# Moving one ScalarE conversion behind four copies in the attention of a two-layer decoder

## The chip, the cores and the metric

The kernel runs on one core of a Trainium2 chip, as one program in one launch. The metric is device time in microseconds (us), the median of several executions; less is better. A separate execution was taken with the hardware profiler, and all rows below come from it.

The engines have short names in the rows. PE is the matrix engine TensorE, and PEld its weight loads, which run beside the matmuls. DVE is VectorE, ACT is ScalarE, POOL is GpSimd, and SP is the engine whose queue issues the weight DMAs. Each engine takes its own instructions strictly in the order in which they were queued, and waits at the first one that isn't ready.

## What is computed

Two layers over 256 positions of width 2048, in float32. Layer 0 is a retention and a short convolution with one input and one output projection. Layer 1, in which the change lies, is windowed attention:

```python
def odd_mixer(h, w_in, q_norm_w, k_norm_w, sinks, w_out, pos):
    proj = h @ w_in
    q, k, v, gate = jnp.split(proj, [ATTN_WIDTH, ATTN_WIDTH + KV_WIDTH, ATTN_WIDTH + 2 * KV_WIDTH], axis=-1)
    q = rope(rms_norm(q.reshape(b, s, ATTN_Q_HEADS, ATTN_HEAD_DIM), q_norm_w), pos)
    k = rope(rms_norm(k.reshape(b, s, ATTN_KV_HEADS, ATTN_HEAD_DIM), k_norm_w), pos)
    o = swa_sinks(q, k, v, sinks).reshape(b, s, ATTN_WIDTH)
    return (o * jax.nn.silu(gate)) @ w_out
```

There are 32 query heads of 64 columns and 4 key/value heads, so four groups of eight query heads share a key head.

## The kernel before

**Products.** Every projection is cut into chunks of 512 output columns, and a chunk into 8 pieces of 256 input rows. A piece is one weight DMA of 512 KB into a tile `raw` (in the rows `woq`, `wog`, `woo` by the chunk's kind: query, gate, output projection). ACT writes its rounded upper part `wh` (`whoq`, `whog`, `whoo`, line 165), DVE the rest `wl = raw - wh` (line 166), and PE adds three products for each of two row blocks and two halves of the piece: 12 matmuls a piece (line 143). The activations are split the same way into an `h` and an `l` tile. There are five buffers each of `raw`, `wh` and `wl`, so ACT converts pieces that PE comes to five pieces later, and the conversion of one piece waits until PE has used the piece five before it.

**Background work.** Work that isn't a projection is written as generators on a list `pending`; after every piece of a chunk, `feed` runs one step of the first of them. So the attention of a group lies in pieces between the products, and all engines take it in that order.

**Layer 1.** The chunks run in the order keys and values, query 0, gate 0, query 1, gate 1, query 2, gate 2, query 3, gate 3, and then the output projection. When a query chunk is done, `attention(g, ...)` (line 589) is put on the list. Its first steps are: the scales `rr` (line 713), then for each row block `t` the turning of the queries, then what an earlier group left over, then the scores.

- `turn_q(t, qs)` (line 594): for each half `j`, PE transposes four heads into a PSUM tile `qt` (line 598), and ACT copies it into `qT[j]` (the rows say `q1T`, line 599). The PSUM tiles `qt` come from the pool `tp`, which has two buffers: the transposes for `t = 1` can't start before the copies for `t = 0` have been read out.
- `finish(j)` (line 747): turns the gated output `og[j]` of a half into the activations of the output projection. ACT writes `ah` (line 749, in the rows `a2h`), and POOL (or, for the last half of all, DVE) writes `al = og - ah` (line 751, `a2l`).
- `late` (line 587): for groups 0 to 2 the second `finish` isn't run by the group itself but left on this list; the next group runs it after its two turnings of queries:

```python
        for t in range(T):
            turn_q(t, qs[t])
            yield
        while late:
            late.popleft()()
        yield
```

The text sets the order only in part. The instructions of the engines are put in a queue by a scheduler, which keeps to what depends on what and otherwise chooses; it queued this conversion on ACT ahead of the copies of the turned queries, though the text runs it behind them. With four groups there are three such places, in the gate chunks of groups 1, 2 and 3. Group 0 goes through the same turning of queries with nothing on `late`.

In the rows `og` is the gated output, whose last step is the multiplication by the gate on DVE (line 709); `gv` is the gate, `qs` the split queries before the turning, `s` the scores, `pt` transposed probabilities, `psog` and `psoq` the PSUM tiles of gate and query chunks.

Of the kernel before, what the change touches and what calls it, by code (L numbers as in the profile page):

```python
# [10 lines left out]
AF = mybir.ActivationFunctionType  # L11
# [46 lines left out]
def hybrid_kernel(  # L58
# [13 lines left out]
    nc = tc.nc  # L72
# [17 lines left out]
    def f32(a):  # L90
        return a.bitcast(F32)
# [474 lines left out]
    def queries(g, ps):  # L566

        rr = op2.tile([P, T, 8], F32, tag="rr", name=f"rr{g}")
        qs, rs = [], []
        for t in range(T):  # L570
            ss = head_ss(f"q{g}{t}", ps[t], 8, t)
            rot = rope1(f"q{g}{t}", "q", ps[t].rearrange("p (h d) -> p h d", h=8), 8, t)
            rs.append(rsqrt_mean(f"q{t}", ss, HD, 8))
            qs.append(split_q(g, t, rot))
        pending.append(attention(g, rr, rs, qs))
# [11 lines left out]
    late = deque()  # L587

    def attention(g, rr, rs, qs):
        ah, al = act2.new()  # L590
        qT = [op2.tile([P, 4, T, P], F32R, tag="qT", name=f"q1T{g}{j}") for j in range(2)]
        mx, pr, nm, es, den = {}, {}, {}, {}, {}

        def turn_q(t, qs):
            for j in range(2):
                tr = tp.tile([P, 4, P], F32R, tag="tp", name=f"qt{g}{t}{j}")
                for h in range(4):
                    nc.tensor.transpose(tr[:, h, :], qs[j][:, h].rearrange("p a d -> p (a d)"), identr)  # L598
                nc.scalar.activation(qT[j][:, :, t, :], f32(tr), AF.Copy)

        def scores(j, h):

# [112 lines left out]
            )  # L715
        yield
        for t in range(T):
            turn_q(t, qs[t])
            yield
        while late:  # L720
            late.popleft()()
        yield
        for j in range(2):
            mx[j] = op2.tile([P, T, 4], F32, tag="mx", name=f"mx{g}{j}")
# [173 lines left out]
```

## Time and profile before

| what | us |
|---|---|
| runs, median of 3 | 803.12 |
| runs, lowest and highest | 802.4 and 803.49 |
| profiled execution, own time | 804.01 |
| its span, first to last instruction | 802.3 |
| PE busy in it | 791.9 (99%) |
| ACT busy in it | 419.5 (52%) |
| DVE busy in it | 501.7 (63%) |
| POOL busy in it | 62.4 (8%) |

The profiled execution took 804.01 us, of which the rows cover the span of 802.3 us; its own time is 0.89 us above the median. Busy time counts an instruction from its start to its modelled end. The matmuls overlap: one starts about 0.23 us after the one before, while each is shown with some 0.39 us. So a short gap between two rows of PE is shorter than what PE lost there, and starts are compared with starts.

### The profile page before, as it was taken

Reading aid. Unit: us, or ns where it says so; the run is one execution under the profiler, and the core shown is the slowest. Engines: PE = TensorE matmul, PEld = TensorE weight load, DVE = VectorE, ACT = ScalarE, POOL = GpSimd, SP = SyncE. Lnnn points to the kernel's source line nnn. Section 1 sums busy time; section 2 is a strip of 40 time slices with the busy share of each in tenths; the row PEclk is TensorE's granted clock in tenths of the full one; section 3 lists DMA queues with packets and bytes.
Section 4 is the critical chain, followed back from the end, with each engine's and each line's share of the span. In section 5 each row is a group of like instructions: output and inputs, shape, how many; then the busy total and the mean of one; then the engine's idle time right before and its main releaser. Section 6 shows DMA issues by size and latency. Waiting matters only on the chain.

```text
span 802.3 us, 10004 instructions
## 1 busy us (share of the span) xinstructions
PE 791.9 (99%) x3660; PEld 654.1 (82%) x3660; DVE 501.7 (63%) x742; ACT 419.5 (52%) x665; POOL 62.4 (8%) x61
## 2 busy tenths in 40 slices
PE   8999999999999999999999999999999999999998
PEld 6888888888888888888888888888878788788886
DVE  6566454664545475445856664877977977777651
ACT  6753434443444434443445443758658678586431
POOL 0000000000000000000000000420500601401000
PEclk9999999999999999999999999999999999999999
DMA  8966645555455655555555555462474454445750
GB/s 310 398 226 229 207 134 185 183 188 197 138 184 190 203 184 183 186 200 192 172 194 176 184 184 193 132 210 84 166 221 132 134 184 157 147 143 174 231 171 26
DMA packets 41088, 147.09 MB, mean 183 GB/s; under 512 B 4560, under 2 KB 4944, under 8 KB 40784
## 3 DMA queue, kind: packets, MB, share of 16 engines
q1 hardware_dynamic: 40752, 146.23, 54.5%
q8 instruction: 28, 0.46, 0.2%
q10 hardware_dynamic: 288, 0.24, 0.2%
q14 instruction: 20, 0.16, 0.1%
HBM read 144.36 MB, written 2.10 MB: 183 GB/s over the span
## 4 chain that ended last, share of the span: by engine, by line
PE 89%; DVE 4%; POOL 3%; issue 2%; ACT 1%; DMA 1%; DVEq 0%; ACTq 0%; POOLq 0%
PE pse L143 44%; PE psoo L143 11%; PE pseo L143 11%; PE psoq L143 10%; PE psog L143 3%; PE psokv L143 3%; POOL rq L225 2%; DVE wlog L166 1%; POOL qs L583 1%; PE pt L674 1%; DVE og L707 1%; DMA sml<-in_small 1%; PE qt L598 1%; PE s L606 0%; DVE og L709 0%
## 5 line engine op out<-in xcount | busy, mean ns | idle before, releaser
L166 DVE TENSOR_TENSOR wle<-we,whe 128x1024 fp32r<-128x1024 f32 (+1 forms) x129 | 156.3, 1217 | 148.6 <-ACT whe L165 148.3
L165 ACT ACTIVATE whe<-we 128x1024 fp32r<-128x1024 f32 (+1 forms) x129 | 135.6, 1052 | 173.9 <-PE pse L143 159.2
L143 PE MATMUL pse<-whe,a0h 128*128 128x512 f32 x512 | 200.0, 396 | 1.3 <-ACT whe L165 1.3
L143 PE MATMUL pse<-whe,a0l 128*128 128x512 f32 x512 | 198.3, 391 | 0.0
L143 PE MATMUL pse<-wle,a0h 128*128 128x512 f32 x512 | 197.8, 390 | 0.0
L143 PEld LDWEIGHTS pse<-whe,a0h 128*128 128x128 f32 x512 | 96.5, 189 | 22.4 <-ACT whe L165 2.9
L143 PEld LDWEIGHTS pse<-whe,a0l 128*128 128x128 f32 x512 | 96.7, 189 | 20.6
L143 PEld LDWEIGHTS pse<-wle,a0h 128*128 128x128 f32 x512 | 96.7, 189 | 19.8
L165 ACT ACTIVATE wheo<-weo 128x1024 fp32r<-128x1024 f32 x32 | 33.9, 1061 | 48.3 <-PE pseo L143 32.7
L166 DVE TENSOR_TENSOR wloo<-woo,whoo 128x1024 fp32r<-128x1024 f32 x32 | 39.5, 1239 | 27.8 <-ACT whoo L165 27.7
L166 DVE TENSOR_TENSOR wleo<-weo,wheo 128x1024 fp32r<-128x1024 f32 x32 | 39.2, 1225 | 27.5 <-ACT wheo L165 27.5
L165 ACT ACTIVATE whoo<-woo 128x1024 fp32r<-128x1024 f32 x32 | 33.9, 1062 | 37.9 <-PE psoo L143 32.7
L166 DVE TENSOR_TENSOR wloq<-woq,whoq 128x1024 fp32r<-128x1024 f32 x32 | 40.0, 1252 | 21.0 <-ACT whoq L165 20.5
L143 PE MATMUL psog<-whog,a1h 128*128 128x512 f32 x128 | 51.0, 398 | 0.0
L143 PE MATMUL psoq<-whoq,a1h 128*128 128x512 f32 x128 | 50.8, 397 | 0.0
L143 PE MATMUL pseo<-wheo,c0h 128*128 128x512 f32 x128 | 50.8, 397 | 0.0
L143 PE MATMUL psog<-wlog,a1h 128*128 128x512 f32 x128 | 50.0, 391 | 0.5 <-DVE wlog L166 0.5
L165 ACT ACTIVATE whoq<-woq 128x1024 fp32r<-128x1024 f32 x32 | 33.9, 1060 | 31.6 <-PE psoq L143 14.0
L143 PE MATMUL psoo<-whoo,a2h 128*128 128x512 f32 x128 | 50.3, 393 | 0.0
L143 PE MATMUL psoq<-wloq,a1h 128*128 128x512 f32 x128 | 50.0, 391 | 0.0
L143 PE MATMUL pseo<-wleo,c0h 128*128 128x512 f32 x128 | 50.0, 390 | 0.0
L143 PE MATMUL psoo<-whoo,a2l 128*128 128x512 f32 x128 | 50.0, 390 | 0.0
(182 smaller groups left out, 1246.3 us busy)
## 6 DMA issues: line engine op xcount, KB each, us to landing
we<-in_w SPq DMA_DIRECT2D x127, 512.0 KB, 3.3
weo<-in_w SPq DMA_DIRECT2D x32, 512.0 KB, 3.2
woq<-in_w SPq DMA_DIRECT2D x32, 512.0 KB, 4.2
wog<-in_w SPq DMA_DIRECT2D x32, 512.0 KB, 3.3
woo<-in_w SPq DMA_DIRECT2D x32, 512.0 KB, 4.2
wokv<-in_w SPq DMA_DIRECT2D x8, 512.0 KB, 3.2
x<-in_xr SPq DMA_DIRECT2D x2, 1024.0 KB, 9.5
out_y<-y SPq DMA_DIRECT2D x7, 256.0 KB, 4.5
```

Of the source, the lines that this page charges most:

```text
L143: nc.tensor.matmul(self.ps[t], self.act(kt)[a][:, t * P : (t + 1) * P], w[:, k * N : (k + 1) * N], start=self.n[t] == 1, stop=self.n[t] == ...
L165: nc.scalar.activation(wh[:, ws], raw[:, ws], AF.Copy)
L166: nc.vector.tensor_tensor(out=wl[:, ws], in0=raw[:, ws], in1=f32(wh[:, ws]), op=ALU.subtract)
L225: nc.gpsimd.tensor_tensor(out=r, in0=v, in1=mhalf[:, :width], op=ALU.pow)
L583: nc.gpsimd.tensor_tensor(out=q[:, :, 1, :], in0=aj, in1=f32(q[:, :, 0, :]), op=ALU.subtract)
L598: nc.tensor.transpose(tr[:, h, :], qs[j][:, h].rearrange("p a d -> p (a d)"), identr)
L674: nc.tensor.transpose(tr[:, h, :], pr[j][:, h, t, :], ident)
L707: nc.vector.tensor_tensor(out=og[half[e], :, ts], in0=o[half[e], :, e, :], in1=sh[half[e]], op=ALU.add)
```

## The change

`turn_q` hands back its last ACT instruction, the copy for `j = 1`, and the left-over work is run inside a block that adds an order without a semaphore: every instruction that the block creates on the engine of `copy` (ACT) is queued behind `copy`. `finish(1)` creates one instruction on ACT, the conversion `a2h`, and one on POOL, `a2l`, which waits for `a2h` in any case.

```diff
                     nc.tensor.transpose(tr[:, h, :], qs[j][:, h].rearrange("p a d -> p (a d)"), identr)
-                nc.scalar.activation(qT[j][:, :, t, :], f32(tr), AF.Copy)
+                copy = nc.scalar.activation(qT[j][:, :, t, :], f32(tr), AF.Copy)
+            return copy.ins
...
         for t in range(T):
-            turn_q(t, qs[t])
+            copy = turn_q(t, qs[t])
             yield
         while late:
-            late.popleft()()
+            with tc.issue_after(copy):
+                late.popleft()()
```

The queues of PE, DVE, POOL and SP hold the same instructions in the same order as before. On ACT three instructions move, one in each of groups 1 to 3. The lines behind the edit are numbered one or two higher afterwards.

ACT's queue in the gate chunk of group 1, before. `whoq_0` to `whoq_3` convert the first pieces of query chunk 2, ahead of their use; `q1T` are the copies of the turned queries of group 1, `a2h` is the left-over conversion of group 0, `sh` a part of its output, `gv` the gate of group 1:

```order
L705 ACTIVATE sh_4599<-ov_4576 64x256 x2
L165 ACTIVATE whoq_0_4752<-woq_0_4751 128x1024
L749 ACTIVATE a2h_4033<-og_4324 128x512
L165 ACTIVATE whoq_1_4793<-woq_1_4792 128x1024
L599 ACTIVATE q1T_4607<-qt_4647 128x4x128
L599 ACTIVATE q1T_4608<-qt_4653 128x4x128
L165 ACTIVATE whoq_2_4832<-woq_2_4831 128x1024
L599 ACTIVATE q1T_4607<-qt_4677 128x4x128
L599 ACTIVATE q1T_4608<-qt_4683 128x4x128
L165 ACTIVATE whoq_3_4880<-woq_3_4879 128x1024
L560 ACTIVATE gv_4744<-psog_0_4530,r1h 128x512
```

The same place of ACT's queue after the change:

```order
L706 ACTIVATE sh_4599<-ov_4576 64x256 x2
L165 ACTIVATE whoq_0_4752<-woq_0_4751 128x1024
L165 ACTIVATE whoq_1_4793<-woq_1_4792 128x1024
L599 ACTIVATE q1T_4607<-qt_4647 128x4x128
L599 ACTIVATE q1T_4608<-qt_4653 128x4x128
L165 ACTIVATE whoq_2_4832<-woq_2_4831 128x1024
L599 ACTIVATE q1T_4607<-qt_4677 128x4x128
L599 ACTIVATE q1T_4608<-qt_4683 128x4x128
L751 ACTIVATE a2h_4033<-og_4324 128x512
L165 ACTIVATE whoq_3_4880<-woq_3_4879 128x1024
L560 ACTIVATE gv_4744<-psog_0_4530,r1h 128x512
```

`a2h` has moved past two weight conversions and four copies, and now stands between the last copy and `whoq_3`. Nothing else changed places.

ACT's queue in the gate chunk of group 3, before, where the pieces converted ahead are those of the first output chunk (`whoo`):

```order
L165 ACTIVATE whoo_0_5902<-woo_0_5901 128x1024
L749 ACTIVATE a2h_5179<-og_5472 128x512
L165 ACTIVATE whoo_1_5943<-woo_1_5942 128x1024
L599 ACTIVATE q1T_5755<-qt_5795 128x4x128
L599 ACTIVATE q1T_5756<-qt_5801 128x4x128
L165 ACTIVATE whoo_2_5982<-woo_2_5981 128x1024
L599 ACTIVATE q1T_5755<-qt_5825 128x4x128
L599 ACTIVATE q1T_5756<-qt_5831 128x4x128
```

And after:

```order
L165 ACTIVATE whoo_1_5943<-woo_1_5942 128x1024
L599 ACTIVATE q1T_5755<-qt_5795 128x4x128
L599 ACTIVATE q1T_5756<-qt_5801 128x4x128
L165 ACTIVATE whoo_2_5982<-woo_2_5981 128x1024
L599 ACTIVATE q1T_5755<-qt_5825 128x4x128
L599 ACTIVATE q1T_5756<-qt_5831 128x4x128
L751 ACTIVATE a2h_5179<-og_5472 128x512
L165 ACTIVATE whoo_3_6030<-woo_3_6029 128x1024
```

The conversion made the same move here.

## Rows read from the trace of the kernel before

**Rows 1.** The profile's page: busy time of each engine, the TensorE clock granted in 40 slices of the span (tenths, 9 is 90% or more), and the shares of the chain of work that ended last.

```profile
PE 791.9 (99%) x3660; PEld 654.1 (82%) x3660; DVE 501.7 (63%) x742; ACT 419.5 (52%) x665; POOL 62.4 (8%) x61
...
PEclk9999999999999999999999999999999999999999
...
PE 89%; DVE 4%; POOL 3%; issue 2%; ACT 1%; DMA 1%; DVEq 0%; ACTq 0%; POOLq 0%
```

**Rows 2.** Who PE waited for, whole program: us in total, times, longest us.

```profile
PE qt L598 <- ACT q1T L599: 3.2, 3, 1.1
PE warm L195 <- DVE zero L192: 1.6, 1, 1.6
PE pse L143 <- ACT whe L165: 1.3, 1, 1.3
PE psog L143 <- DVE wlog L166: 0.5, 1, 0.5
```

**Rows 3.** PE in order of time, in the gate chunk of group 1 around the turning of the queries: start us, us, engine, line, operation, output and inputs, count, and in brackets the idle time before and what ended it. The row of 584.81 is the last matmul of the chunk's sixth piece, that of 587.13 the first of its seventh.

```profile
581.36 0.39 PE L143 MATMUL psog<-whog,a1l 128*128 128x512 f32 x1
581.59 0.79 PE L598 MATMUL qt<-identr,qs 128*128 128x128 f32 x8
...
584.81 0.39 PE L143 MATMUL psog<-whog,a1l 128*128 128x512 f32 x1
586.29 1.00 PE L598 MATMUL qt<-identr,qs 128*128 128x128 f32 x8 [1.09 <-ACT q1T L599]
587.13 0.47 PE L143 MATMUL psog<-whog,a1h 128*128 128x512 f32 x1
```

**Rows 4.** The same view in the gate chunks of groups 2 and 3.

```profile
639.79 0.39 PE L143 MATMUL psog<-whog,a1l 128*128 128x512 f32 x1
641.25 0.99 PE L598 MATMUL qt<-identr,qs 128*128 128x128 f32 x8 [1.07 <-ACT q1T L599]
642.08 0.47 PE L143 MATMUL psog<-whog,a1h 128*128 128x512 f32 x1
...
694.71 0.39 PE L143 MATMUL psog<-whog,a1l 128*128 128x512 f32 x1
696.17 1.00 PE L598 MATMUL qt<-identr,qs 128*128 128x128 f32 x8 [1.07 <-ACT q1T L599]
697.01 0.47 PE L143 MATMUL psog<-whog,a1h 128*128 128x512 f32 x1
```

**Rows 5.** ACT in order of time, in the gate chunk of group 1. The four `whoq` rows from 579.06 on are `whoq_0` to `whoq_3`, the two `q1T` rows the pairs of copies for `t = 0` and `t = 1`.

```profile
579.06 1.06 ACT L165 ACTIVATE whoq<-woq 128x1024 fp32r<-128x1024 f32 x1 [0.30 <-PE psog L143]
584.08 0.63 ACT L749 ACTIVATE a2h<-og 128x512 fp32r<-128x512 f32 x1 [3.96 <-DVE og L709]
584.62 1.04 ACT L165 ACTIVATE whoq<-woq 128x1024 fp32r<-128x1024 f32 x1
585.57 1.07 ACT L599 ACTIVATE q1T<-qt 128x512 fp32r<-128x512 f32 x2
586.53 1.05 ACT L165 ACTIVATE whoq<-woq 128x1024 fp32r<-128x1024 f32 x1
587.47 1.08 ACT L599 ACTIVATE q1T<-qt 128x512 fp32r<-128x512 f32 x2
590.23 1.06 ACT L165 ACTIVATE whoq<-woq 128x1024 fp32r<-128x1024 f32 x1 [1.67 <-issue]
592.22 1.37 ACT L560 ACTIVATE gv<-psog,r1h 128x512 f32<-128x512 f32 x2 [0.93 <-PE psog L143]
```

**Rows 6.** Who ACT waited for, whole program, one row of it: us in total, times, longest us.

```profile
ACT a2h L749 <- DVE og L709: 11.8, 3, 4.0
```

**Rows 7.** DVE in order of time at the same place. The rows of line 166 are the rests of the last three gate pieces and of `whoq_0`, `whoq_1` and `whoq_3`.

```profile
578.41 2.89 DVE L166 TENSOR_TENSOR wlog<-wog,whog 128x1024 fp32r<-128x1024 f32 x2
...
582.22 1.23 DVE L166 TENSOR_TENSOR wlog<-wog,whog 128x1024 fp32r<-128x1024 f32 x1
583.37 0.68 DVE L709 TENSOR_TENSOR og<-og,gT 128x512 f32<-128x512 f32 x1
583.97 1.22 DVE L166 TENSOR_TENSOR wloq<-woq,whoq 128x1024 fp32r<-128x1024 f32 x1
585.70 1.70 DVE L166 TENSOR_TENSOR wloq<-woq,whoq 128x1024 fp32r<-128x1024 f32 x1 [0.51 <-ACT whoq L165]
...
591.32 1.23 DVE L166 TENSOR_TENSOR wloq<-woq,whoq 128x1024 fp32r<-128x1024 f32 x1 [2.48 <-ACT whoq L165]
```

**Rows 8.** PE and then ACT in order of time at the turning of the queries of group 0, where nothing is left over.

```profile
531.10 0.39 PE L143 MATMUL psog<-whog,a1l 128*128 128x512 f32 x1
531.33 0.80 PE L598 MATMUL qt<-identr,qs 128*128 128x128 f32 x8
531.97 0.47 PE L143 MATMUL psog<-whog,a1h 128*128 128x512 f32 x1
...
531.58 1.06 ACT L165 ACTIVATE whoq<-woq 128x1024 fp32r<-128x1024 f32 x1 [0.97 <-PE psog L143]
```

**Rows 9.** Who the weight loads of PE waited for, whole program, one row of it.

```profile
PEld qt L598 <- issue: 4.4, 3, 1.5
```

**Rows 10.** POOL in order of time, from the split of the queries of group 1 to its next work behind `a2l`.

```profile
577.73 2.49 POOL L583 TENSOR_TENSOR qs<-aq,qs 128x256 fp32r<-128x256 f32 x2
584.79 1.52 POOL L751 TENSOR_TENSOR a2l<-og,a2h 128x512 fp32r<-128x512 f32 x1 [4.57 <-ACT a2h L749]
611.33 0.64 POOL L685 TENSOR_SCALAR_AFFINE_SELECT uh<-ph 128x512 fp32r<-128x512 f32 x1 [25.02 <-ACT ph L678]
```

**Rows 11.** SP in order of time: the weight DMAs for `woq_1` and `woq_2` being issued; and the time from issue to landing of the DMAs of `woq` between 560 and 600 us.

```profile
567.78 0.33 SPq L164 DMA_DIRECT2D woq<-in_w  x1
579.68 0.33 SPq L164 DMA_DIRECT2D woq<-in_w  x1
...
DMA to landing us min/median/max: 3.7/4.5/4.9
```

**Rows 12.** Two pieces of the chain that ended last, in order of time: start us, us, what. They are the fourth piece of query chunk 2, the first that uses `whoq_3`, and the fifth piece of the first output chunk, the first that reads `a2h` and `a2l` of group 2.

```profile
603.95 2.75 PE psoq L143 x12
...
717.02 2.79 PE psoo L143 x12
```

## The prediction

> **What bounds the kernel now.** I read the page first. PE is busy for 791.9 of 802.3 us at the full clock in every slice (the 2.4 GHz level), and the chain that ended last lies on PE for 89% [rows 1]. So an edit on ACT is worth what PE stands still for, and nothing else. The next view is therefore who PE waited for. In the whole program there are four lines, and the longest is the one that touches this change: the transposes of the turned queries (line 598) waited three times for the copies on ACT (line 599), 3.2 us together [rows 2]. The third view is the order of time on PE around one of them, in the gate chunk of group 1: the transposes for `t = 0` follow the matmul ahead of them without a gap, those for `t = 1` come at 586.29, with 1.09 us idle ahead, put down to `q1T` [rows 3]. Groups 2 and 3 show the same with 1.07 us [rows 4].
>
> The fourth view says why the copies were late. ACT ended `whoq_0` at 580.12 and then stood for 3.96 us, until DVE had finished `og`, since `a2h` was at the head of its queue. Only then came `whoq_1` and, at 585.57, the first copies [rows 5]. That wait is there three times, 11.8 us in all [rows 6]. The fifth view, DVE, shows why `og` is late: its last step stands behind three weight rests and ends at 583.37 + 0.68 = 584.05 [rows 7]. So the chain is DVE `og`, ACT `a2h`, `whoq_1`, copies, PE transposes. A control stands in the same trace: group 0 has nothing left over, and its second transposes follow at 531.33, 0.23 us after the matmul ahead [rows 8].
>
> **What the wait costs.** Idle time on PE's row isn't the loss, since matmuls overlap. I take start to start, from the last matmul of the sixth piece to the first of the seventh. Group 1: 587.13 - 584.81 = 2.32 us [rows 3]. Groups 2 and 3: 642.08 - 639.79 = 2.29 and 697.01 - 694.71 = 2.30 [rows 4]. Group 0, without a wait: 531.97 - 531.10 = 0.87 [rows 8]. The excess is 1.45 + 1.42 + 1.43 = 4.30 us. It is more than three idle gaps (1.09 + 1.07 + 1.07 = 3.23 [rows 3, 4]) because the transposes themselves spread out, 1.00 instead of 0.80 us, while they wait for the second copy.
>
> The weight loads give a second measure: those of the transposes stood for 4.4 us in three waits [rows 9]. The Trainium skill, Perfetto Trace Analysis, section Identifying the Most-Contended Engine, says that the busy share of matmuls is a poor measure for PE, because pipelined instructions look different in the trace, and that the busy share of the weight loads should be used instead. By PE's own row the gain would end at 3.2 us, by that rule at 4.4; the starts, which are neither, agree with the rule.
>
> **Removed.** The wait of `a2h` ahead of `whoq_1`. What releases `whoq_1` next? Its buffer is that of the fifth gate piece, whose last matmul starts at 581.36 and is shown for 0.39 [rows 3], so 581.75. In group 0 a conversion that waited for PE started at 531.58, against 531.10 + 0.39 = 531.49 [rows 8], so I add 0.09: 581.84. Its weights were issued at 567.78 and land in 3.7 to 4.9 us [rows 11], long before. `whoq_1` takes 1.04, and the two copies end 586.64 - 584.62 = 2.02 after its start [rows 5], so 583.86. The transposes that they read are done by 581.59 + 0.79 = 582.38 [rows 3]. The second transposes can start at 584.81 + 0.23 = 585.04 as in group 0, and the last copy is out 1.18 us before. So the whole excess should go, not a part of it.
>
> **Moved.** `a2h` goes behind `whoq_2` and the second copies. `whoq_2` waits for the sixth piece: 584.81 + 0.39 + 0.09 = 585.29. Its weights, issued at 579.68, land by 584.2 to 584.6 [rows 11]: some 0.7 us of cover, and if that is gone the copies behind it slip, which nothing reads before the chunk is done; its gate starts at 592.22 - 1.45 = 590.8 [rows 5], 3.4 us later. It takes 1.05, the copies are over 587.47 + 1.08 - 586.53 = 2.02 after its start [rows 5], at 587.31, and `a2h` comes at about 587.2, long after `og` is ready at 584.05. It adds 584.62 - 584.08 = 0.54 us to the queue [rows 5], to 587.8. Behind it stand `whoq_3` and the gate `gv`. `whoq_3` started at 590.23 after 1.67 us of idle time [rows 5]; 1.45 us earlier that is 588.78, so `a2h` lies in idle time with 1 us to spare. If that cover weren't there, it would cost from 0 to 3 x 0.54 = 1.6 us; I take 0, because PE needs `whoq_3` only at 603.95 [rows 12], and its rest ends at 591.32 + 1.23 [rows 7].
>
> `a2l` on POOL follows 0.71 us after the start of `a2h` and takes 1.52 [rows 10], so it ends near 589.5. POOL's next work is at 611.33 [rows 10], so nothing queues behind it. The readers of `a2h` and `a2l` are the output chunks: for group 2, whose conversion moves to 587.2 + 697.01 - 587.13 = 697.1 [rows 3, 4] on the old times, the first is at 717.02 [rows 12]. Also held longer, by about 3 us, is the buffer of `og`; no instruction between there and 611.33 on POOL's queue needs it. On DVE the rest of `whoq_1` took 1.70 us beside `a2l`, against 1.22 for the one ahead [rows 7, 10]; `a2l` will now lie in the 2.5 us in which DVE waits for `whoq_3`. Neither way does PE see it. SP's queue has no new entry; the weight DMAs that wait for `wloq_1` go out about 1 us earlier.
>
> **What is late next.** Behind each place the next wait of PE in layer 1 before was at the next place [rows 2], and what ACT and DVE do in between is started by PE's chunks, so it moves with PE. I expect the full 4.30 us to arrive at the end.
>
> **The sum.** The profiled execution's own time is 804.01 us, its span 802.3. 804.01 - 4.30 = 799.7, with a span near 798.0. Against the median of the runs, 0.89 us lower: 803.12 - 4.30 = 798.8 us, 0.54% faster.
>
> **The rivals.**
>
> *Only part comes.* The copies could come early and PE still wait, for a semaphore from the copies or for `whoq_1` starting later than PE's fifth piece allows. For it: `whoq_1` was never seen without `a2h` ahead of it. Against it: group 0 has the same queue and no gap [rows 8], and 1.18 us are to spare. Half the excess left gives 803.12 - 2.15 = 801.0 us. Chance 0.08.
>
> *It doesn't do what it says, or it comes back.* The wait named could have been another: if `whoq_1` were released at about 584.6 by something that the row doesn't name, the copies come when they came before, and the time stays at 803.1. Or DVE and POOL, whose chain of `og`, rests and split queries between two chunks is long, hold PE later for what was gained. Against the first stands the row itself, which names DVE's `og`, and `og` ends 0.03 us before `a2h` starts; against the second, that the split queries for `t = 1` are done at 577.73 + 2.49 = 580.2 [rows 10], nearly 5 us before their transposes, and the rests of the gate pieces at 583.4 [rows 7], before PE's seventh piece at 585.7. Chance 0.05, 803.1 us.
>
> *Slower: the wait moves with the instruction.* `a2h` at its new place is again the head of ACT's queue; if `og` weren't ready there, `whoq_3`, the gate and the copies of the scores would stand behind it. If PE then paid the whole wait of ACT (3.96 us, three times, instead of the 1.45 that reach it now), the time would be 803.12 + 11.9 - 4.3 = 810.7 us. It decides from the point where `og` ends later than `whoq_3` can start, 588.8; the row has `og` at 584.05 [rows 7], 4.7 us before, and DVE's work ahead of it isn't touched. Chance 0.02.
>
> **How the numbers follow.** The forecast has 0.85, the rivals 0.08, 0.05 and 0.02. About 0.2% (1.6 us) is what a measurement of this kernel can tell from no change; forecast and the first rival lie beyond it: faster 0.93, same 0.05, slower 0.02. For the range I take the two bounds of the excess against the spread of the runs of before: 802.4 - 4.4 = 798.0, and 803.49 - 3.23 = 800.3.
>
> **What would show it.** Right: PE's wait for `q1T` is gone from the list of waits, start to start at the three places is 0.87 us, `a2h` has no wait for `og`, `whoq_1` starts right after the fifth piece, ACT idles before `whoq_3` for about 1 us, the span is near 798.0. Wrong: a gap of PE before the second transposes that names something other than a copy (part only); an idle time of ACT before `a2h` (slower); new lines of waits of PE in layer 1 that add up to what was gained (it comes back).

## The result and the profile after

| | before | after |
|---|---|---|
| median of 6 runs each, us | 803.32 | 799.02 |
| lowest and highest, us | 802.4 and 803.84 | 797.76 and 799.53 |
| profiled execution, own time, us | 804.01 | 798.12 |
| its span, us | 802.3 | 796.4 |

The changed kernel is faster by 4.30 us; the ratio is 0.9944, with a 95% interval from 0.9931 to 0.9957. The forecast was 798.8 us, a gain of 4.30, with a range from 798.0 to 800.3.

Who PE waited for, whole program, in the changed kernel (us in total, times, longest us):

```profile
PE warm L195 <- DVE zero L192: 1.5, 1, 1.5
PE pse L143 <- ACT whe L165: 1.4, 2, 0.9
PE psog L143 <- DVE wlog L166: 0.5, 1, 0.5
```

Against [rows 2] one line is gone, the wait of the turning transposes for the copies, and no new one stands in layer 1. PE in order of time around the second transposes of groups 1, 2 and 3 (start us, us, engine, line, operation):

```profile
583.28 0.39 PE L143 MATMUL psog<-whog,a1l 128*128 128x512 f32 x1
583.51 0.79 PE L598 MATMUL qt<-identr,qs 128*128 128x128 f32 x8
584.14 0.47 PE L143 MATMUL psog<-whog,a1h 128*128 128x512 f32 x1
...
636.79 0.39 PE L143 MATMUL psog<-whog,a1l 128*128 128x512 f32 x1
637.02 0.79 PE L598 MATMUL qt<-identr,qs 128*128 128x128 f32 x8
637.65 0.47 PE L143 MATMUL psog<-whog,a1h 128*128 128x512 f32 x1
...
690.29 0.39 PE L143 MATMUL psog<-whog,a1l 128*128 128x512 f32 x1
690.53 0.79 PE L598 MATMUL qt<-identr,qs 128*128 128x128 f32 x8
691.16 0.47 PE L143 MATMUL psog<-whog,a1h 128*128 128x512 f32 x1
```

From the last matmul of the sixth piece to the first of the seventh it is now 0.86, 0.86 and 0.87 us, where [rows 3, 4] had 2.32, 2.29 and 2.30, and group 0 had 0.87 [rows 8]. The three differences are 1.46 + 1.43 + 1.43 = 4.32 us. ACT in order of time at the place in group 1:

```profile
580.26 1.06 ACT L165 ACTIVATE whoq<-woq 128x1024 fp32r<-128x1024 f32 x1 [1.66 <-PE psog L143]
581.22 1.07 ACT L599 ACTIVATE q1T<-qt 128x512 fp32r<-128x512 f32 x2
583.71 1.06 ACT L165 ACTIVATE whoq<-woq 128x1024 fp32r<-128x1024 f32 x1 [1.42 <-PE psog L143]
584.68 1.07 ACT L599 ACTIVATE q1T<-qt 128x512 fp32r<-128x512 f32 x2
585.63 0.63 ACT L751 ACTIVATE a2h<-og 128x512 fp32r<-128x512 f32 x1
587.21 1.06 ACT L165 ACTIVATE whoq<-woq 128x1024 fp32r<-128x1024 f32 x1 [0.94 <-ACT a2h L751]
```

The two weight conversions now wait for PE, 1.66 and 1.42 us, as that of group 0 did; the first copies end at 582.29, 1.22 us before the second transposes start. `a2h` has no idle time ahead of it, so `og` was ready, and 0.94 us are left behind it before `whoq_3`.

The two profiled executions differ by more than the change: their spans by 5.9 us. The rest was there before any edited place. The first transposes of group 0, where both kernels do the same, started at 527.88 before and at 526.36 after, 1.52 us apart. From there to the end of the span it is 802.3 - 527.88 = 274.42 and 796.4 - 526.36 = 270.04 us. The difference of 4.38 is what the change is worth in the profiles, and agrees with the three places to 0.06 us.

### The profile page after: what moved, and what is told of

It is laid out like the page before. It is cut to its first block, busy times and chain, and to the rows that moved or that the text cites. A ratio compares the mean times of both kernels' runs of the same rounds, so it can differ in the third digit from the quotient of the medians.

```text
span 796.4 us, 10004 instructions
## 1 busy us (share of the span) xinstructions
PE 789.2 (99%) x3660; PEld 652.4 (82%) x3660; DVE 500.0 (63%) x742; ACT 419.9 (53%) x665; POOL 61.7 (8%) x61
## 4 chain that ended last, share of the span: by engine, by line
PE 96%; POOL 1%; DVE 1%; DMA 1%; issue 0%; SPq 0%; ACT 0%; DVEq 0%; POOLq 0%
PE pse L143 44%; PE pseo L143 11%; PE psoo L143 11%; PE psoq L143 10%; PE psog L143 10%; PE psokv L143 3%; PE pt L675 1%; DMA we<-in_w 1%; PE ov L698 1%; PE ov L697 1%; POOL rq L225 1%; PE qt L598 1%; PE s L607 0%; PE s L610 0%; PE s L609 0%; PE gt L666 0%
## 5 line engine op out<-in xcount | busy, mean ns | idle before, releaser
L143 PE MATMUL psoq<-whoq,a1l 128*128 128x512 f32 x128 | 50.0, 390 | 0.0
```

What stands on the lines that cost most here:

```text
L143: nc.tensor.matmul(self.ps[t], self.act(kt)[a][:, t * P : (t + 1) * P], w[:, k * N : (k + 1) * N], start=self.n[t] == 1, stop=self.n[t] == ...
```

## The experiments

Theory: PE pays for the wait of `a2h` for `og`, by way of `whoq_1` and the first two copies, at three places that don't depend on each other. Rivals: the gain comes from somewhere else or the places hang together; what costs is the work or place of `a2h` on ACT, not its wait; all four copies must be ahead of it; there is no room at the old or at the new place. Kernels that ran together share the runs of the kernel before: 803.37 us (median) beside the first four, 803.05 beside the last two.

### One place alone

```diff
-            with tc.issue_after(copy):
+            if g == 1:
+                with tc.issue_after(copy):
+                    late.popleft()()
+            else:
                 late.popleft()()
```

> The conversion is queued behind the copies in group 1 alone; in groups 2 and 3 it stays ahead of them. Theory (PE loses 1.45, 1.42 and 1.43 us at three places, each by itself): group 1 shows 0.87 us from the last matmul of the sixth piece to the first of the seventh, groups 2 and 3 still 2.3 us, and the time is about 803.3 - 1.45 = 801.9 us. Rival (the places hang together, what is gained at one is lost at the next): groups 2 and 3 grow beyond 2.3 us and the time stays at 803.3. Rival (the gain has another source, in the start of the kernel): the time is near 799 or near 803.3, whatever the places show.

Measured: 801.77 us, ratio 0.9982 (0.9973 to 0.9991), 1.6 us less than before. Who PE waited for, whole program, one row of it:

```profile
PE qt L598 <- ACT q1T L599: 2.2, 2, 1.1
```

PE in order of time on both sides of the second transposes of groups 1, 2 and 3:

```profile
584.22 0.39 PE L143 MATMUL psog<-whog,a1l 128*128 128x512 f32 x1
...
585.08 0.47 PE L143 MATMUL psog<-whog,a1h 128*128 128x512 f32 x1
...
637.73 0.39 PE L143 MATMUL psog<-whog,a1l 128*128 128x512 f32 x1
...
640.02 0.46 PE L143 MATMUL psog<-whog,a1h 128*128 128x512 f32 x1
...
692.64 0.39 PE L143 MATMUL psog<-whog,a1l 128*128 128x512 f32 x1
...
694.95 0.47 PE L143 MATMUL psog<-whog,a1h 128*128 128x512 f32 x1
```

Two of the three waits are back. Group 1 shows 0.86 us, groups 2 and 3 show 2.29 and 2.31, as before the change. What one place gains isn't lost at the next: the one that was changed gave its own 1.45 us. The 95% interval of the time runs from 801.2 to 802.6 us, which leaves out both 799 and 803.3, so the start of the kernel isn't where the gain comes from.

### Behind the first two copies only

```diff
-            copy = turn_q(t, qs[t])
+            copies.append(turn_q(t, qs[t]))
...
-            with tc.issue_after(copy):
+            with tc.issue_after(copies[0]):
```

> The conversion is queued behind the first pair of copies only, ahead of the next weight conversion and the second pair. Theory (only what stands ahead of the first pair counts, since the second transposes need just these two copies): the conversion waits some 0.2 us for the gated output and then lies in the idle time before the next weight conversion; the three places show 0.87 us, time 799.0 as with the full change. Rival (all four copies must be ahead of it): an excess is left at the places, the time lies between 800 and 802 us.

Measured: 799.32 us, ratio 0.9947 (0.9935 to 0.996), the same as the full change within the intervals. All three places show 0.86 to 0.87 us. ACT in order of time in group 1:

```profile
582.30 1.06 ACT L599 ACTIVATE q1T<-qt 128x512 fp32r<-128x512 f32 x2
583.63 0.63 ACT L752 ACTIVATE a2h<-og 128x512 fp32r<-128x512 f32 x1 [0.27 <-DVE og L710]
584.78 1.06 ACT L165 ACTIVATE whoq<-woq 128x1024 fp32r<-128x1024 f32 x1 [0.52 <-PE psog L143]
```

`a2h` waits for `og` again, 0.27 us, and nobody pays, because ACT would otherwise have waited for PE. So what decides is what stands behind a waiting instruction, and only `whoq_1` and the first pair of copies, which wait behind it, were urgent. That the full change also moves `a2h` past `whoq_2` and the second pair is worth nothing measurable.

### The output earlier, the queue of ACT unchanged

```diff
-                nc.vector.tensor_tensor(out=og, in0=og, in1=gT, op=ALU.mult)
+                gate_mult[g] = nc.vector.tensor_tensor(out=og, in0=og, in1=gT, op=ALU.mult).ins
...
+                if pc == NP - 1 and self.name in ("og1", "og2", "og3"):
+                    with tc.issue_after(gate_mult[int(self.name[2]) - 1]):
+                        parts = self.split(pc, fine)
+                else:
+                    parts = self.split(pc, fine)
...
```

`gate_mult` is a dictionary that starts empty, and `parts` goes to the products as the result of `split` did. The rest is the kernel before, without the change.

> Nothing is moved on ACT: the conversion stays ahead of the copies, as before. On VectorE the last step of the gated output goes ahead of one weight rest, so that it ends about 1.15 us earlier. Theory (the wait for that output is what PE pays for): the conversion starts about 1.13 us earlier, the second copy ends at a point where the second transposes wait for some 0.3 us instead of 1.45; excess at the three places 0.1 to 0.4 us each, time about 803.3 - 3 x 1.15 = 799.9 us. Rival (it is the work or the place of the conversion on ACT that costs, not its wait): excess and time as before, 803.3 us.

Measured: 799.32 us, ratio 0.9952 (0.9938 to 0.9966). ACT, then PE in order of time in group 1:

```profile
581.08 0.63 ACT L755 ACTIVATE a2h<-og 128x512 fp32r<-128x512 f32 x1 [2.83 <-DVE og L715]
581.62 1.05 ACT L171 ACTIVATE whoq<-woq 128x1024 fp32r<-128x1024 f32 x1
582.57 1.07 ACT L605 ACTIVATE q1T<-qt 128x512 fp32r<-128x512 f32 x2
...
582.94 0.39 PE L149 MATMUL psog<-whog,a1l 128*128 128x512 f32 x1
583.30 0.99 PE L604 MATMUL qt<-identr,qs 128*128 128x128 f32 x8
584.13 0.46 PE L149 MATMUL psog<-whog,a1h 128*128 128x512 f32 x1
```

The wait of `a2h` is 2.83 us instead of 3.96, and the place shows 584.13 - 582.94 = 1.19 us instead of 2.32 (groups 2 and 3: 1.17 each). `a2h` stands where it stood and does the same work: a wait shorter by 1.13 us took 1.13 us from PE at this place. So the loss follows the wait, with place and work unchanged, and neither of them alone was the price. It doesn't say that the work costs nothing at the old place: the 0.32 us that are left there are less than the 0.54 us that the conversion adds to the queue.

### More work ahead of the second transposes

```diff
-                copy = nc.scalar.activation(qT[j][:, :, t, :], f32(tr), AF.Copy)
+                for _ in range(4 if g and t == 0 and j == 0 else 1):
+                    copy = nc.scalar.activation(qT[j][:, :, t, :], f32(tr), AF.Copy)
```

On top of the full change; the second kernel has 3 in the place of 4.

> The full change, and in groups 1 to 3 the first copy is done three more times over the same data, right behind the first pair. Each repeat waits for the one before it, about 0.65 us. Theory (the copies have 1.18 us to spare): the buffer is free about 0.7 us after the second transposes could start, or 0.35 if it is that of the later half, so each place shows 1.2 to 1.6 us instead of 0.87 and the time is 800.1 to 801.1 us. Rival (there is more to spare than I worked out): 799.0 us.

> The full change, with two repeats of the first copy instead of three. Theory (1.18 us to spare): the second repeat ends just as the second transposes could start; each place shows 0.87 to 1.0 us, time 799.0 to 799.4 us. Rival (any work ahead of the second transposes is paid): 2 x 0.55 us at each place, 802.3 us.

Measured: 800.7 us with three repeats, ratio 0.9968 (0.9955 to 0.9981), and 798.27 with two, ratio 0.994 (0.9927 to 0.9954). The second lies below the 799.0 to 799.4 us expected, but its interval, 797.2 to 799.4 us, covers them. With three, ACT and PE in order of time in group 1:

```profile
581.99 2.81 ACT L600 ACTIVATE q1T<-qt 128x512 fp32r<-128x512 f32 x5
...
584.04 0.39 PE L143 MATMUL psog<-whog,a1l 128*128 128x512 f32 x1
584.27 0.46 PE L598 MATMUL qt<-identr,qs 128*128 128x128 f32 x4
584.95 0.50 PE L598 MATMUL qt<-identr,qs 128*128 128x128 f32 x4 [0.22 <-ACT q1T L600]
585.29 0.46 PE L143 MATMUL psog<-whog,a1h 128*128 128x512 f32 x1
```

With two repeats, ACT in order of time in group 1:

```profile
582.29 2.19 ACT L600 ACTIVATE q1T<-qt 128x512 fp32r<-128x512 f32 x4
```

With two, the copies end at 584.48, the second transposes start at 584.58 as if nothing were there, and the place shows 0.86 us. With three they end at 584.80. The first half of the transposes is on time and the second half, whose buffer is held, comes 0.15 us after that end; the place shows 1.25 us, an excess of 0.38. Without the repeats the pair of copies would have ended at 581.99 + 1.07 = 583.06, so the three add 584.80 - 583.06 = 1.74 us, of which 0.38 are paid. The second transposes therefore have room for about 1.74 - 0.38 = 1.36 us of work ahead of them, and the next 0.6 us is paid in part. I had worked out 1.18 us to the start of the transposes; the rest fits what the PE rows show, that the first half starts on time and only the second half waits for the last buffer.

### More work at the new place

```diff
-            nc.scalar.activation(ah[:, ks, :], og[j], AF.Copy)
+            for _ in range(4 if j and g < 3 else 1):
+                nc.scalar.activation(ah[:, ks, :], og[j], AF.Copy)
```

On top of the full change.

> The full change, with the moved conversion done four times over the same data: three times ahead of the next weight conversion, once behind it, some 2 us of ACT's time more at each place. Theory (at its new place the conversion lies in idle time, and the weights behind it are needed more than 10 us later): the next weight conversion starts up to 0.4 us later, PE shows no new wait, time 799.0 us. Rival (the new place is on PE's path as the old one was): up to 2 us at each place, 801 to 805 us.

Measured: 798.14 us, ratio 0.9941 (0.9928 to 0.9953), as the full change. ACT in order of time in group 1:

```profile
586.24 1.96 ACT L752 ACTIVATE a2h<-og 128x512 fp32r<-128x512 f32 x3
588.11 1.04 ACT L165 ACTIVATE whoq<-woq 128x1024 fp32r<-128x1024 f32 x1
589.06 0.62 ACT L752 ACTIVATE a2h<-og 128x512 fp32r<-128x512 f32 x1
589.82 1.37 ACT L560 ACTIVATE gv<-psog,r1h 128x512 f32<-128x512 f32 x2
```

The idle time behind the copies is filled to the last, `whoq_3` and the gate start without a wait of their own, and the three places on PE show 0.86 to 0.87 us. Four conversions fit there at no cost that PE shows.

### All of them from the same point

The start of the kernel differs from execution to execution, so I compare the profiles from the first transposes of group 0 to the end of the span. "Expected" is 270.04 plus the excess that PE's three places show over 0.87 us each.

| kernel | first transposes, us | span, us | difference | expected |
|---|---|---|---|---|
| before | 527.88 | 802.3 | 274.42 | 274.3 |
| after | 526.36 | 796.4 | 270.04 | |
| one place | 527.29 | 800.2 | 272.91 | 272.9 |
| first copies only | 527.42 | 797.6 | 270.18 | 270.0 |
| output earlier | 526.01 | 797.0 | 270.99 | 271.0 |
| three extra copies | 527.12 | 798.4 | 271.28 | 271.2 |
| two extra copies | 527.41 | 797.5 | 270.09 | 270.0 |
| load at the new place | 526.98 | 797.2 | 270.22 | 270.0 |

All agree within about 0.2 us, with spans that the profile gives to 0.1 us: nothing larger than that is left in any of them that PE's three places don't account for.

## Why the prediction was right

- **The bound.** PE was the engine to look at, and the wait of line 598 the only one in reach: it disappeared, and PE's list shows nothing in its place in layer 1.
- **The size.** The sum went by starts, 4.30 us. Measured are 4.30 between the medians, 4.32 at the three places and 4.38 between the profiles from a common point. That the medians meet the sum to the hundredth is luck: their interval allows a gain of 3.5 to 5.5 us. It is the three places that show the size. The three idle gaps, 3.23 us, would have fallen short by a quarter. The prediction puts the difference down to the transposes that spread out, but in group 1 that is only 1.00 - 0.80 = 0.20 of 1.45 - 1.09 = 0.36 us; the other 0.16 is that a matmul is shown with 0.39 us while the next can start after 0.23. The 4.4 us in which the weight loads stood [rows 9] were the nearer of the two. The section Identifying the Most-Contended Engine in the Trainium skill's Perfetto Trace Analysis prefers the weight loads for the busy share of PE; that their waits also size a gap better is what this case shows, not the page.
- **What releases the copies next.** `whoq_1` was expected 0.09 us after the fifth piece is shown to end, and the copies 1.18 us before they are needed. They came 1.22 us before, near enough. The two kernels with extra copies put the room at about 1.36 us, somewhat more than the working had, since it asked for both buffers at the start of the transposes.
- **The moved conversion.** Expected at no wait and about 1 us of room; the row has 0.94. No price of it shows on PE at the new place, nor of three more; the comparison from the common point would show one above some 0.2 us.
- **The rivals.** That only part comes was ruled out by the places, which are at group 0's level. That it comes back was ruled out by one place alone: groups 2 and 3 didn't grow. That the wait moves with the instruction happens in small in the kernel with the first copies only, 0.27 us, and costs nothing there.
- **What isn't explained.** The start of the kernel moved the two profiles apart by another 1.52 us (below), so the span of 796.4 us came out 1.6 below the 798.0 that the prediction named as a sign. It isn't the change's: the place is ahead of all edited ones, and the medians don't have it.

## What to carry to other kernels

When the engine that sets the time waits for a short instruction, look in that engine's queue for the first idle time ahead of it and ask what stood at the head: here a conversion that nobody needed for the next 20 us and more waited 3.96 us for its input, with the urgent copies behind it. It is enough to move it past the urgent ones, into a stretch in which the queue waits for the bounding engine anyway; and a gap on a pipelined engine is to be sized from start to start, against the same place without the wait.

## What the runs showed of the hardware

**VectorE and GpSimd hold each other up.** Moving `a2h` also moves POOL's `a2l`, and where that ends up changes DVE. In the kernel with the first copies only, POOL, then DVE in order of time in group 1:

```profile
584.34 1.55 POOL L754 TENSOR_TENSOR a2l<-og,a2h 128x512 fp32r<-128x512 f32 x1 [4.58 <-ACT a2h L752]
...
583.51 1.22 DVE L166 TENSOR_TENSOR wloq<-woq,whoq 128x1024 fp32r<-128x1024 f32 x1
584.65 2.32 DVE L166 TENSOR_TENSOR wloq<-woq,whoq 128x1024 fp32r<-128x1024 f32 x1
```

The rest that began during `a2l` took 2.32 us instead of 1.22: it ended at 586.97, 1.08 us after `a2l` did, as if it had started only then. It goes the other way round too: `a2l` itself began before the rest ahead had ended (583.51 + 1.22 = 584.73), took 1.55 us instead of the 1.29 of the full change, and ended 1.16 us after that rest. In the kernel with more work at the new place it began at 589.75, beside a rest that took 1.22 us and ended at 590.41; there `a2l` took 1.82 us and ended 1.16 us after the rest as well. In each of these meetings the one that began second was the one that took longer. In the full change the two don't meet. DVE and POOL there, in order of time:

```profile
582.44 3.60 DVE L166 TENSOR_TENSOR wloq<-woq,whoq 128x1024 fp32r<-128x1024 f32 x3
...
586.34 1.29 POOL L753 TENSOR_TENSOR a2l<-og,a2h 128x512 fp32r<-128x512 f32 x1 [7.65 <-ACT a2h L751]
```

The three rests are over at 582.44 + 3.60 = 586.04, 1.2 us each, before `a2l` starts. The section Who interferes with whom of SBUF — State Buffer in the Trainium skill has this: a VectorE instruction with two inputs from the SBUF contends with a GpSimd instruction that reads it. PE saw none of it: its three places show 0.86 to 0.87 us in both kernels.

**The start.** The first matmuls of the kernel ran at two speeds. PE in order of time, before and then after:

```profile
6.68 2.07 PE L143 MATMUL pse<-whe,a0h 128*128 128x512 f32 x4 [1.35 <-ACT whe L165]
8.55 1.91 PE L143 MATMUL pse<-whe,a0l 128*128 128x512 f32 x4
```

```profile
6.27 1.25 PE L143 MATMUL pse<-whe,a0h 128*128 128x512 f32 x4 [0.94 <-ACT whe L165]
7.36 1.07 PE L143 MATMUL pse<-whe,a0l 128*128 128x512 f32 x4
```

Four matmuls took 8.55 - 6.68 = 1.87 us in the one execution and 7.36 - 6.27 = 1.09 in the other, in code that is the same in both; the granted clock between 6 and 12 us is shown as 1.00 in both. The kernel with the first copies only has such a slow stretch too, a little later. PE there, in order of time:

```profile
9.40 1.91 PE L143 MATMUL pse<-wle,a0h 128*128 128x512 f32 x4
11.11 1.14 PE L143 MATMUL pse<-whe,a0h 128*128 128x512 f32 x4
```

Four matmuls took 11.11 - 9.40 = 1.71 us, and here the granted clock is shown as 0.50 from 8 to 11 us, the lower of the two levels (1.2 GHz). So the slow stretch before is probably the same level, which its profile doesn't show; no run settles that. Six of the eight profiles have such a stretch. The two without it, after and output earlier, have the two earliest first transposes of group 0, which came between 526.01 and 527.88 us. Between before and after the difference is complete early: the 41st matmul on PE, warm-up matmuls counted, starts at 15.54 us after and 1.53 us later before, and at the first transposes of group 0 it is still 1.52 us. What makes the start go one way or the other wasn't tried; it is a spread of 1.9 us in single profiles that has to be taken off before two of them are compared.
